# Moving eight weight-sum steps ahead of a bias load, and loading the bias in one transfer

## The chip, the cores and the metric

The kernel runs on one core of a Trainium2 chip. The metric is the device time of one execution in microseconds (us). Three timed runs of the kernel before the change stand beside one execution that was profiled; the times in the trace are counted from the start of its span.

## The reference

One layer of a transformer trunk on 512 tokens of width 2048, in float32: a norm, sliding-window attention with a learned bias by distance, an output projection, and a gated embedding. Cut to what matters here:

```python
hn = rmsnorm(x, norm_g)
q, k, v, gate = split(hn @ w_in)             # 32 query heads, 4 key heads, head width 64
bias = rel_bias[bucket(query - key)]         # 32 buckets x 32 heads
scores = q @ k.T * 64 ** -0.5 + bias         # a query sees 128 keys
probs = softmax over the seen keys and one sink per head
x = x + ((probs @ v) * silu(gate)) @ w_out
x = x + (p @ ple_proj) * sigmoid(rmsnorm(x) @ ple_gate)
return rmsnorm(x, final_g)
```

## The kernel before

Every float32 product is made from three matmuls on halves that TensorE takes at full rate: the high part of a weight times both parts of the activation, and the low part of the weight times the high part (`mm3`, L112, issued at L124 to L126). One step of such a product over 128 input channels is called a k-step here: three matmuls of 128x512.

The program has these stages. First the norm and the first columns of the input projection, one input block of 128 channels after the other (L177 to L246, tiles `xr`, `w0`, `w0s`, results `qps`, `ktps`, `vps`). Then the rest of the input projection, 30 column blocks of 16 k-steps each, run by a generator `proj`: the first 32 k-steps in a loop of four times eight, the others spread between the steps of the attention (L942 to L1008). Then the output projection, the gate and the last norm.

The weights of the generator come in pieces of 128x1024 (512 KB). `Weights.load` (L98) issues the read of a piece `wraw` on the queue of SP (the sync engine). ACT (ScalarE) rounds it to the high part `whi` (L107) and DVE (VectorE) subtracts to get `wlo` (L113). There are three buffers of each. A piece feeds eight k-steps, so 24 matmuls. Pieces are counted from 0 here; pieces 0 to 2 are read at the end of the first stage, and piece 3 is the first one behind the bias load on SP's queue.

The bias of the attention is a table by distance. POOL (GpSimd) reads `rel_bias` into the tile `misc` (L320), lays its columns out by distance with 17 copies (L324, L329), and writes the result to the DRAM tile `tdram` (L331). `load_bias(kv)` (L373) then reads the rows of one group of eight heads back, shifted per query, into the tile `bias`; `load_bias(0)` (L927) stands ahead of the first loop and waits for `tdram`, the others are issued inside the attention. The first use of the bias is `biased(0)` on DVE (L439).

The later projections use a scheme with fewer products that needs sums of weight blocks. They are made in DRAM during the attention by `sum_weights(i)` (L648): an even `i` issues a copy of a 512 KB block from DRAM to DRAM on SP's queue (L652), an odd `i` issues the accumulating transfer that adds a second block onto an earlier copy, on POOL's queue (L654), three copies behind. So of the steps 0 to 7, four issue copies (steps 0, 2, 4, 6) and one issues an accumulation (step 7). Below, C0, C1 ... are the copies and A0, A1 ... the accumulations, in their order; A0 waits until C0 has landed. Steps 0 to 7 stand in the first loop, two after every eight k-steps; the rest is spread over the attention.

The instruction order on TensorE and SP is that of the program text throughout. From the line ahead of `load_bias(0)` on, the order of POOL, DVE and ACT is the program's too; in the text ahead of it, which holds the building of the bias table, a scheduler orders those three by when it takes an instruction to be ready, and it may set instructions of the later text in front of earlier ones.

Of the kernel before, what the change touches and what calls it, by code (L numbers as in the profile page):

```python
# [20 lines left out]
P = 128  # L21
# [7 lines left out]
GROUP = HEADS // KVH  # L29
HB = P // 2  # L30
QB = P // GROUP
# [8 lines left out]
TOEP = 384  # L40
# [15 lines left out]
def trunk_kernel(ctx: ExitStack, tc: tile.TileContext, a: dict):  # L56
    nc = tc.nc
# [128 lines left out]
    for k in range(KC):  # L186
# [10 lines left out]
        h = room.tile([P, S], F32R, tag="ah", name=f"xh{k}")  # L197
# [127 lines left out]
    for b in range(exact, BUCKETS):  # L325
        d = np.nonzero(bk == b)[0]
        if len(d):
            lo, n = P - 1 + int(d.min()), len(d)
            nc.gpsimd.tensor_copy(tvec[:, lo : lo + n], relb[:, b : b + 1].to_broadcast([HEADS, n]))  # L329
    tdram = tc.dram_tile([HEADS, TOEP], F32, name="tdram")  # L330
# [12 lines left out]
    U, T, PT, O, gates, biases = {}, {}, {}, {}, {}, {}  # L343
# [28 lines left out]

    def load_bias(kv):  # L373
        biases[kv] = apool.tile([P, P + HB], F32, tag="bias", name=f"bias{kv}", bufs=2)
        for h in range(GROUP):
            src = bass.AP(
                tensor=tdram.tensor, offset=tdram.offset + (GROUP * kv + h) * TOEP + HB, ap=[[1, QB], [1, P + HB]]
            )
            nc.sync.dma_start(biases[kv][QB * h : QB * h + QB], src)

    def where(i):

# [4 lines left out]
    def scores(i):  # L387

        kv, j, g, s = where(i)
        if j == 8 and kv + 1 < KVH:
            load_bias(kv + 1)
        key = K[kv]
        q = Q[i // 4]
        s_ps = SP[i] = spsum.tile([P, 2, S], F32, tag="w", name=f"s{i}")
        n = (HB, P)[g] if g < 2 else P + QB
        for u in range(2):
            st = q[:, (2 * i + u) % (P // QB)].rearrange("p h q -> p (h q)")
            first = 0 if g < 2 else (g - 2) * HB + (s + u) * QB  # L400
            nc.tensor.matmul(s_ps[:, u, : 2 * n], st, key[:, :, first : first + n], start=True, stop=True)  # L401
# [214 lines left out]
    def large_sum(nm, p, only=range(2)):  # L616
        for jj in only:
            for m in range(4):
                first = {7: (1, 2), 5: (1, 1)}.get(p)
                summed[nm, p, jj, m] = sum_of(  # L620
                    block(nm, *first, jj, m) if first else summed[nm, 7 if p == 6 else 6, jj, m],
                    block(nm, *{7: (2, 2), 5: (1, 2), 6: (1, 1), 4: (2, 1)}[p], jj, m),
                    f"{nm}_{p}_{jj}_{m}",
                )
# [17 lines left out]
    large_sum("ple_gate", 5, (0,))  # L642
    small_sum(4, 4, lambda i: small[4, 6, i], lambda i: large_piece(1, 0, i))
    large_sum("ple_gate", 5, (1,))
    SUM_START = 8
    SUM_REST = 2 * len(copies) + 6 - SUM_START

    def sum_weights(i):  # L648

        if i % 2 == 0 and i // 2 < len(copies):  # L650
            if copies[i // 2]:
                nc.sync.dma_start(*copies[i // 2])  # L652
        elif i % 2 == 1 and 0 <= i // 2 - 3 < len(adds):
            nc.gpsimd.dma_start(*adds[i // 2 - 3], accum_op=ALU.add, max_dma_last_dim=8192)  # L654
# [247 lines left out]
    def projections():  # L902
# [21 lines left out]
            engines={getattr(mybir.EngineType, v) for v in ("PE", "SP", "Pool", "DVE", "Activation")}  # L924
        )
    )
    load_bias(0)  # L927
    blocks = KVH * STEPS
    at = 0

    def ksteps(n):
        nonlocal at
        for _ in range(n):
            while len(W.made) <= min(at // 8, len(W.srcs) - 1):
                W.split()
            at += 1
            next(proj)

    def splits(ahead):
        return len(W.made) <= min(at // 8 + ahead, len(W.srcs) - 1)  # L940

    for n in range(2 * 2):  # L942
        while splits(2):
            W.split()
        ksteps(8)
        for v in range(SUM_START // 4):
            sum_weights(n * (SUM_START // 4) + v)
    for e in range(2):
        for lo in (False, True):
            make_q(0, e, lo)  # L950
# [8 lines left out]
    for i in range(blocks + 3):  # L959
# [46 lines left out]
        if i < blocks:  # L1006
            for n in range(i * SUM_REST // blocks, (i + 1) * SUM_REST // blocks):
                sum_weights(SUM_START + n)  # L1008
    while W.open:
# [453 lines left out]
    n = done[3]  # L1463
# [87 lines left out]
```

## Time and profile before

| what | value |
|---|---|
| median of three timed runs | 791.01 us (790.99 to 791.08) |
| the profiled execution | 791.13 us |
| its span, first to last instruction | 789.4 us |
| mean granted TensorE clock | 0.998 |
| TensorE busy in the span | 779.7 us (99%) |
| VectorE, ScalarE, GpSimd busy | 613.5, 499.4, 174.4 us |
| HBM traffic over the span | 327 GB/s |

The profiled execution is 1.73 us longer than its span. Times in the trace are starts; "SPq" and "POOLq" are the queues from which an engine issues transfers. A transfer's time to landing runs from its issue to the moment the waiting engine may go on. Matmuls overlap: each has a duration of about 0.39 us in the trace while the next one starts 0.23 us after it, so starts are what counts.

### The profile page before, as it was taken

To read this page: it belongs to the slowest core of one execution; us is meant where nothing else is said; L and a number is where in the kernel's file an instruction comes from. 1 tells how busy PE (TensorE), PEld (TensorE's weight loads), DVE (VectorE), ACT (ScalarE), POOL (GpSimd) and SP (SyncE) were. 2 spreads that over 40 slices of the span, in tenths; PEclk is the share of its full clock that TensorE was granted. 3 is DMA by queue.
4 is the path that set the end of the run, shared out by engine and by line. 5 is a ranking of instruction groups with operands and counts; after the bars stand their busy time and mean duration, and the time that the engine had idled before them with its cause. 6 is when DMAs were issued, how large, how long until landed. Compare 5 with 4: busy or idle time off the path is not lost.

```text
span 789.4 us, 11241 instructions
## 1 busy us (share of the span) xinstructions
PE 779.7 (99%) x3738; PEld 651.6 (83%) x3738; DVE 613.5 (78%) x1043; ACT 499.4 (63%) x1015; POOL 174.4 (22%) x382
## 2 busy tenths in 40 slices
PE   9999999999999999999999999999999999999995
PEld 7888888888888888888888888888888888888885
DVE  4436478888877788687887798999788757899886
ACT  5632377667566666565666656767679756666755
POOL 0012413554244414542243200100000120200000
PEclk9999999999999999999999999999999999999999
DMA  8791999999999998999999597997783996885533
GB/s 336 276 225 41 315 279 289 253 300 282 327 277 268 255 276 242 240 256 278 281 282 220 154 321 252 269 380 265 239 298 101 358 225 227 163 215 192 178 107 107
DMA packets 48778, 194.41 MB, mean 246 GB/s; under 512 B 7328, under 2 KB 8480, under 8 KB 42992
## 3 DMA queue, kind: packets, MB, share of 16 engines
q1 hardware_dynamic: 39600, 148.81, 53.3%
q0 software_dynamic: 8688, 44.36, 29.7%
q8 instruction: 29, 0.48, 0.3%
q10 hardware_dynamic: 432, 0.52, 0.2%
q14 instruction: 29, 0.24, 0.1%
HBM read 187.85 MB, written 70.31 MB: 327 GB/s over the span
## 4 chain that ended last, share of the span: by engine, by line
PE 98%; DMA 1%; ACT 0%; DVE 0%; SPq 0%; issue 0%; ACTq 0%; DVEq 0%
PE gps L124 7%; PE gps L125 7%; PE gps L126 7%; PE qps L126 7%; PE qps L124 7%; PE qps L125 7%; PE o L125 6%; PE o L126 6%; PE o L124 6%; PE g L124 6%; PE g L125 6%; PE g L126 6%; PE s L401 2%; PE o L523 2%; PE vps L228 2%; PE pt L479 2%
## 5 line engine op out<-in xcount | busy, mean ns | idle before, releaser
L124 PE MATMUL gps<-xh,whi 128*128 128x512 f32 x256 | 100.4, 392 | 0.0
L125 PE MATMUL gps<-xl,whi 128*128 128x512 f32 x256 | 100.0, 391 | 0.0
L126 PE MATMUL gps<-xh,wlo 128*128 128x512 f32 x256 | 99.8, 390 | 0.0
L503 POOL TENSOR_SCALAR_AFFINE_SELECT own<-r 64x256 fp32r<-64x256 f32 x96 | 60.9, 634 | 165.1 <-ACT r L484 82.7
L113 DVE TENSOR_TENSOR wlo<-wraw,whi 128x1024 fp32r<-128x1024 f32 x60 | 74.0, 1235 | 24.0 <-ACT whi L107 22.5
L124 PE MATMUL qps<-xh,whi 128*128 128x512 f32 x224 | 87.5, 391 | 0.0
L125 PE MATMUL qps<-xl,whi 128*128 128x512 f32 x224 | 87.5, 390 | 0.0
L126 PE MATMUL qps<-xh,wlo 128*128 128x512 f32 x224 | 87.3, 390 | 0.0
L461 ACT ACTIVATE t<-t,sm 128x129 f32<-128x129 f32 x128 | 50.7, 397 | 49.6 <-DVE sm L452 46.8
L124 PE MATMUL g<-bhi,fhg 128*128 128x512 f32 x192 | 75.2, 391 | 0.0
L125 PE MATMUL g<-blo,fhg 128*128 128x512 f32 x192 | 74.7, 389 | 0.0
L126 PE MATMUL g<-bhi,flg 128*128 128x512 f32 x192 | 74.7, 389 | 0.0
L107 ACT CAST whi<-wraw 128x1024 fp32r<-128x1024 f32 x60 | 62.2, 1038 | 15.0 <-DMA wraw<-in_w_q 8.8
L689 ACT CAST bhi<-braw 128x1024 fp32r<-128x1024 f32 x44 | 46.3, 1054 | 36.0 <-PE g L126 19.4
L690 DVE TENSOR_TENSOR blo<-braw,bhi 128x1024 fp32r<-128x1024 f32 x44 | 54.0, 1228 | 18.6 <-ACT bhi L689 18.5
L690 DVE TENSOR_TENSOR blo<-ring,bhi 128x1024 fp32r<-128x1024 f32 x48 | 58.3, 1221 | 6.5 <-ACT bhi L689 6.1
L689 ACT CAST bhi<-ring 128x1024 fp32r<-128x1024 f32 x48 | 50.3, 1051 | 20.4 <-PE o L126 16.6
L484 ACT CAST r<-pt 128x256 fp32r<-128x256 f32 x64 | 23.8, 372 | 54.8 <-PE pt L479 54.4
L126 PEld LDWEIGHTS gps<-xh,wlo 128*128 128x128 f32 x256 | 48.1, 188 | 10.5
L124 PEld LDWEIGHTS gps<-xh,whi 128*128 128x128 f32 x256 | 48.1, 188 | 9.1
L125 PEld LDWEIGHTS gps<-xl,whi 128*128 128x128 f32 x256 | 48.1, 188 | 8.7
L671 POOL DMA_DIRECT2D grown<-in_ple_gate x16 | 13.7, 854 | 176.3 <-DMA grown<-ple_gate 119.7
(263 smaller groups left out, 1985.3 us busy)
## 6 DMA issues: line engine op xcount, KB each, us to landing
w_out<-in_w_out POOLq DMA_DIRECT2D x32, 512.0 KB, 8.6
wraw<-in_w_gate_in SPq DMA_DIRECT2D x32, 512.0 KB, 6.9
ring<-w_out SPq DMA_DIRECT2D x32, 512.0 KB, 5.5
wraw<-in_w_q SPq DMA_DIRECT2D x28, 512.0 KB, 8.3
braw<-in_ple_gate SPq DMA_DIRECT2D x24, 512.0 KB, 4.4
ring<-in_w_out SPq DMA_DIRECT2D x18, 512.0 KB, 4.5
w_out<-in_w_out SPq DMA_DIRECT2D x16, 512.0 KB, 9.1
w_out<-w_out SPq DMA_DIRECT2D x16, 512.0 KB, 13.5
```

The lines of the kernel that those rows point to most:

```text
L107: nc.scalar.copy(hi, self.raw[i])
L113: nc.vector.tensor_sub(lo, raw, hi.bitcast(F32))
L124: nc.tensor.matmul(ps, sh, mh, start=first, stop=False, skip_group_check=more)
L125: nc.tensor.matmul(ps, sh, ml, start=False, stop=False, skip_group_check=more)
L126: nc.tensor.matmul(ps, sl, mh, start=False, stop=last, skip_group_check=more)
L228: nc.tensor.matmul(v_ps[t], h[:, c], both[:, :, 256:512], start=f, stop=e, skip_group_check=True)
L401: nc.tensor.matmul(s_ps[:, u, : 2 * n], st, key[:, :, first : first + n], start=True, stop=True)
L461: nc.scalar.activation(su, su, AF.Exp, bias=sm[:, u : u + 1], accum_out=sm[:, 2 + u : 3 + u])
L484: nc.scalar.copy(r[:, 0], PT[i])
L503: nc.gpsimd.affine_select(out=cols(own[places[g % 2 ^ low]]), in_=cols(r[here, low].bitcast(F32)), pattern=[[sign * QB, 2], [0, GROUP], [s ...
L689: nc.scalar.copy(hi, raw)
L690: nc.vector.tensor_sub(lo, raw, hi.bitcast(F32))
```

## The change

`load_bias` issues one transfer for the 128 rows of a group where it issued eight of 16 rows each. Steps 0 to 7 of `sum_weights` go in front of `load_bias(0)`; the first loop issues steps 8 to 15 where it issued steps 0 to 7, and the part spread over the attention is shorter by eight steps.

```diff
     def load_bias(kv):
         biases[kv] = apool.tile([P, P + HB], F32, tag="bias", name=f"bias{kv}", bufs=2)
-        for h in range(GROUP):
-            src = bass.AP(
-                tensor=tdram.tensor, offset=tdram.offset + (GROUP * kv + h) * TOEP + HB, ap=[[1, QB], [1, P + HB]]
-            )
-            nc.sync.dma_start(biases[kv][QB * h : QB * h + QB], src)
+        src = bass.AP(
+            tensor=tdram.tensor, offset=tdram.offset + GROUP * kv * TOEP + HB, ap=[[TOEP, GROUP], [1, QB], [1, P + HB]]
+        )
+        nc.sync.dma_start(biases[kv], src)
...
-    SUM_START = 8
+    SUM_FIRST, SUM_START = 8, 16
     SUM_REST = 2 * len(copies) + 6 - SUM_START
...
+    for n in range(SUM_FIRST):
+        sum_weights(n)
     load_bias(0)
...
         ksteps(8)
-        for v in range(SUM_START // 4):
-            sum_weights(n * (SUM_START // 4) + v)
+        for v in range((SUM_START - SUM_FIRST) // 4):
+            sum_weights(SUM_FIRST + n * ((SUM_START - SUM_FIRST) // 4) + v)
```

The order of the instructions on TensorE, DVE and ACT is the same in both kernels. It differs on SP and on POOL.

SP's queue at the end of the first stage, before: three pieces of weights are read, then the bias, then pieces 3 and 4, and the copies of the weight sums (`small`) come after those.

```order
L101 DMA wraw_683<-in_w_q 128x1024
L379 DMA bias_810<-tdram 16x192 x8
L101 DMA wraw_823<-in_w_q 128x1024
L101 DMA wraw_829<-in_w_q 128x1024
L652 DMA small_7_0_746<-in_w_out 16x8192
L101 DMA wraw_861<-in_w_q 128x1024
L652 DMA small_7_1_747<-in_w_out 16x8192
```

The same place after (lines of the changed text are one or two lower):

```order
L101 DMA wraw_683<-in_w_q 128x1024
L651 DMA small_7_0_746<-in_w_out 16x8192
L651 DMA small_7_1_747<-in_w_out 16x8192
L651 DMA small_5_0_748<-in_w_out 16x8192
L651 DMA small_5_1_749<-in_w_out 16x8192
L378 DMA bias_815<-tdram 128x1x192
L101 DMA wraw_821<-in_w_q 128x1024
L101 DMA wraw_827<-in_w_q 128x1024
L651 DMA w_out_0_0_750<-in_w_out 16x8192
```

C0 to C3 stand ahead of the bias now, and the bias is one row instead of eight.

POOL at the same time, before: the spread of the norm's factors (`rb`), then the table in `misc`. Its write to `tdram` follows 13 rows further down, and A0 right behind that.

```order
L242 DMA rb<-rdram 128x512
L320 DMA misc<-in_rel 32x32
L321 MEMSET misc 32x384
L324 COPY misc<-misc 32x16
L329 COPY misc<-misc 32x3
L329 COPY misc<-misc 32x2
```

And after:

```order
L242 DMA rb<-rdram 128x512
L653 DMA small_7_0_746<-in_w_out 64x2048
L653 DMA small_7_1_747<-in_w_out 64x2048
L653 DMA small_5_0_748<-in_w_out 64x2048
L653 DMA small_5_1_749<-in_w_out 64x2048
L320 DMA misc<-in_rel 32x32
L321 MEMSET misc 32x384
L324 COPY misc<-misc 32x16
```

Four accumulations, A0 to A3, stand ahead of the building of the table. Only A0 belongs to the steps that the text puts in front of `load_bias(0)`; A1 to A3 come from the first loop, and the scheduler has set all four ahead of the read of `rel_bias`. The rest of the table is as before, and A4 follows the write to `tdram` where A0 followed it.

## The prediction

> **What bounds the kernel now.** I read the page's busy shares and chain first, then the windows around the changed place, then SP's waits and the timelines of SP, POOL, ACT, DVE and PE between 49 and 105 us.
>
> ```profile
> PE 779.7 (99%) x3738; PEld 651.6 (83%) x3738; DVE 613.5 (78%) x1043; ACT 499.4 (63%) x1015; POOL 174.4 (22%) x382
> PE 98%; DMA 1%; ACT 0%; DVE 0%; SPq 0%; issue 0%; ACTq 0%; DVEq 0%
> ```
>
> TensorE is busy for 779.7 of 789.4 us and carries 98% of the chain. No transfer and no other engine holds it up anywhere between the first load and the tail. So nothing that only shortens work on SP, POOL or the DMA engines can shorten the run; a step that makes TensorE wait lengthens it by that wait.
>
> The windows (columns PE, PEld, DVE, ACT, POOL busy, granted clock, DMA share, GB/s) show what lies fallow at the changed place:
>
> ```profile
> 59.00:60.00 1.00, 1.00 (x6) 0.78 (x6) 1.00 (x2) 1.00 (x2) 1.00 (x1) 1.00 0.25 102
> 60.00:65.00 5.00, 5.00 (x25) 4.21 (x24) 4.08 (x5) 2.19 (x3) 4.64 (x6) 1.00 0.00 2
> 65.00:70.00 5.00, 5.00 (x25) 4.17 (x24) 1.76 (x5) 0.00 (x0) 0.00 (x0) 1.00 0.06 13
> 70.00:75.00 5.00, 5.00 (x26) 4.17 (x25) 4.95 (x11) 1.65 (x3) 0.00 (x0) 1.00 0.06 14
> ```
>
> The DMA engines run dry at about 59.25 (a quarter of that us) and stand still to 75 while TensorE goes on at full clock. SP's waits and its queue say why:
>
> ```profile
> SPq L379 <- DMA tdram<-misc: 14.8, 1, 14.8
> SPq L379 <- PE vps L228: 5.3, 1, 5.3
> 49.58 1.81 SPq L101 DMA_DIRECT2D wraw<-in_w_q  x3
> 71.69 3.88 SPq L379 DMA_DIRECT2D bias<-tdram  x8
> 75.60 0.90 SPq L101 DMA_DIRECT2D wraw<-in_w_q  x2
> 76.55 0.60 SPq L652 DMA_DIRECT2D small<-in_w_out  x1
> ```
>
> SP is free at 51.39, waits 14.8 us for the table (to 66.2), then 5.3 us for the last `vps` matmul, whose weights lie where the bias goes. Piece 3 of the weights is queued behind that bias.
>
> **The slack of piece 3.** PE's first matmul on piece 0, its first on piece 3, and the split of piece 3:
>
> ```profile
> 71.49 0.40 PE L124 MATMUL qps<-xh,whi 128*128 128x512 f32 x1
> 87.83 0.39 PE L124 MATMUL qps<-xh,whi 128*128 128x512 f32 x1
> 79.59 1.05 ACT L107 CAST whi<-wraw 128x1024 fp32r<-128x1024 f32 x1 [5.98 <-DMA wraw<-in_w_q]
> 80.67 1.23 DVE L113 TENSOR_TENSOR wlo<-wraw,whi 128x1024 fp32r<-128x1024 f32 x1 [4.82 <-ACT whi L107]
> ```
>
> 72 matmuls take 16.34 us, 0.227 each. Piece 3 is issued at 75.60, lands at 79.5 (3.9 later), `wlo` is done at 81.9 (2.4 later). PE wants `wlo` with its third matmul, 0.45 after the first, so piece 3 is ready for a start at 81.45 and is wanted at 87.83: 6.4 us of slack.
>
> **The change part by part.** The bias in one transfer:
>
> ```profile
> L379 SPq DMA_DIRECT2D bias<-tdram x32: 302/418/676, 71.7 to 308.5; - x32
> ```
>
> Eight issues took 3.88 us; for one I take the median of 0.42 (least 0.30, most 0.68). It gives piece 3 some 3.4 us. The later three bias loads save issue time on SP too, and since PE waits for nothing there, that is worth nothing. Steps 8 to 15 in place of 0 to 7 and the shorter rest: the same instructions earlier, on queues PE does not wait for; nothing.
>
> The copies in front: C0 to C3 go out from 51.39 on, while SP would only wait, so their issue costs nothing. What they cost lies on POOL. A0 to A3 stand ahead of the table there, each waits for its copy, and behind them wait the table, `tdram`, the bias on SP and piece 3. POOL before:
>
> ```profile
> 49.71 0.53 POOL L320 DMA_DIRECT2D misc<-in_rel  x1
> 57.40 0.19 POOL L324 COPY misc<-misc 32x16 f32<-32x16 f32 x1 [6.73 <-DMA misc<-in_rel]
> 64.42 0.51 POOL L331 DMA_DIRECT2D tdram<-misc  x1 [0.29 <-POOL misc L329]
> 83.67 0.86 POOL L654 DMA_DIRECT2D small<-in_w_out  x1 [18.74 <-DMA wraw<-in_w_q]
> ```
>
> Step one, the copies. Three transfers in a row (C0, piece 5, C1, issued at 76.55, 77.19, 77.81) landed after
>
> ```profile
> DMA to landing us min/median/max: 6.8/6.8/6.8
> DMA to landing us min/median/max: 7.6/7.6/7.6
> DMA to landing us min/median/max: 8.0/8.0/8.0
> ```
>
> that is at 83.35, 84.79 and 85.81: one per 1.23 us. Starting at 59.25 with about 1 us to land, C0 lands at 61.5, and alone C1 to C3 would at 62.7, 64.0, 65.2; their data are out at 64.2. POOL took A0 up 0.3 us after C0 landed (83.67). So A0 is issued at 61.8, and A3 at about 66.
>
> Step two, the accumulations. They come one after the other on POOL's transfer queue. The trace has a stretch where little else ran than such transfers (into SBUF, L671, window 630 to 650, columns packets, MB, share of 16 engines):
>
> ```profile
> q0 software_dynamic: 1077, 3.95, 99.6%
> q0 software_dynamic: 8688, 44.36, 29.7%
> ```
>
> 19.9 us for 3.95 MB is 2.64 us per block of 0.524 MB; over the whole run (second row) it is 2.77. I take 2.7, nearest to both. With 0.86 us of issue and some 0.8 to the first byte (an estimate: the 5.1 us that the quickest of the L671 transfers needs, less 0.86, 2.64 and 0.8 to land), A0 moves from 63.4. Then 0.85 us of copies and 4 x 2.7 us of accumulations are left for the same DMA engines: done at 75.05, landed at 75.95.
>
> ```profile
> DMA to landing us min/median/max: 5.1/5.3/5.4
> rb<-rdram POOLq DMA_DIRECT2D x1, 256.0 KB, 7.6
> misc<-in_rel POOLq DMA_DIRECT2D x1, 4.0 KB, 7.6
> ```
>
> Step three, the table. `misc` is 4 KB, and still needed 7.6 us behind the 256 KB `rb` issued 0.57 us before it: it landed 0.57 after `rb`. I read that as a queue that goes in order. So `misc` lands at 76.5, not 57.4. From there to `tdram` landing took 8.8 us (57.4 to 66.2): 85.3. The bias adds 0.42; piece 3 is issued at 85.75, lands at 89.65, and is ready for a start at 91.6. PE wants it at 87.83: it waits 3.8 us.
>
> **Sum.** In short, wait = landing of `misc` - 72.75, and nothing below 72.75. 789.4 + 3.8 = 793.2 of span, with 1.73 around it 794.9 for the profiled execution; from the median of 791.01, 0.12 lower, 794.8.
>
> What is late next: A4 stands behind `tdram` on POOL and waits for C4, now behind pieces 3 and 4 on SP. C0 was issued 0.95 after piece 3 and landed 6.8 later; so C4 lands at 93.5.
>
> ```profile
> 88.88 0.74 POOL L355 TENSOR_TENSOR values<-values 64x256 f32<-64x256 f32 x1
> 100.18 0.76 DVE L302 TENSOR_TENSOR diffs<-diffs 128x256 fp32r<-128x256 f32 x2 [0.53 <-ACT diffs L301]
> ```
>
> From A0's start to the end of the key differences POOL took 5.95 us (83.67 to 89.62), so they are done at 99.5; DVE wants them at 100.18 + 3.8 = 104. That cover of 4.5 us holds. Piece 4 lands some 1.5 us behind piece 3 and is wanted 5.4 behind it. No second wait.
>
> **A page against a row.** The Trainium skill (DMA: Bandwidth & Descriptors, "Anatomy of one DMA — SWDGE (gpsimd) path") prices a POOL transfer at 2.0 us plus its bytes at 436 GB/s. By that a block moves in 1.2 us once the first is under way (an estimate from that page), the sum would be no wait and 791.0, and the change would be free. The row of 2.64 us is what this kernel measured for accumulating transfers, and I go by it.
>
> **The rivals.** *B, no wait.* The accumulations run at the pace of plain transfers, 1.23 us, or `misc` isn't held by them. Then A3, issued at 65.5, moves at 67.2 and is landed at 69.2; `misc` lands at 69.8, 3 us inside the point of 72.75. Everything stays hidden: 791.0. It decides where one accumulation costs under some 1.8 us. For it speaks that the queues are empty between 60 and 75, against it the 2.64. The page's rule above would make this the outcome. Chance 0.15.
>
> *C, a long wait and the clock.* Copies and accumulations disturb each other: were the copies to need 2.64 each as well, work would end at 59.25 + 8 x 2.64 = 80.4, `misc` land at 81.9 and PE wait 9.1 us. The clock then matters. After the last matmul, at 780.5, the windows have
>
> ```profile
> 784.00:785.00 1.00, 0.00 (x0) 0.00 (x0) 0.86 (x3) 0.59 (x1) 0.00 (x0) 1.00 0.54 176
> 785.00:786.00 1.00, 0.00 (x0) 0.00 (x0) 0.00 (x0) 0.13 (x1) 0.00 (x0) 0.94 1.03 345
> 786.00:787.00 1.00, 0.00 (x0) 0.00 (x0) 0.00 (x0) 0.00 (x0) 0.00 (x0) 0.50 1.05 357
> 780.54 0.28 PE L126 MATMUL e<-bhi,pTl 128*128 128x256 f32 x1
> 0.85 3.66 PE L145 MATMUL warm_ps<-const-bfloat16-1.0 128*128 128x128 bf16 x34 [0.85 <-PEq L1541]
> ```
>
> a full clock for 5.1 us and half of it from 785.9 on. How long it stays at half, no row shows; the warm-up of 3.66 us at the start is the nearest, and half a clock for that long loses 1.8. In the forecast PE stands idle for 2.7 us, then 0.8 for `wlo`, and the clock holds. With `misc` at 79.3 the wait is 6.5 and the clock goes: 791.0 + 6.5 + 1.8 = 799.3. At 9.1 it would be 801.9. Chance 0.10. The Trainium skill (TensorE: Matmul & The Clock Gate, "What's actually happening") puts the fall after one idle window of about 3.4 us, earlier than the 5.1 seen here; by it a wait only little above my forecast would already pay.
>
> *D, faster.* Merged bias issues and earlier sums would have to free time on PE. There is none to free in the rows. Chance 0.03, for something not in the profile.
>
> **How the numbers follow.** The forecast (wait of 1.6 to 6) has 0.72 and gives 794.8. About 0.2%, 1.6 us, is what a measurement of this kernel tells from no change; B lies within it, D below, the forecast and C above: faster 0.03, same 0.15, slower 0.82. Low is 790.9, since B is cheap to reach and the accumulations' price, 1.23 to 2.77, spans 791 to 795.1; high is 800.0, C at its likelier place.
>
> **What would show it.** Right: POOL's first L324 copy near 76.5, `bias` issued on SP near 85.3, a gap of 3 to 4 us in PE's row near 88, with the releaser `whi` or `wlo`, and all PE starts behind it late by that much, the DMA share near 1 from 60 to 75. Wrong: L324 before 72.7 (B), a PEclk below 1 near 90 (C), a first L324 as early as 57, or a second PE gap between 95 and 115 (POOL's key differences).

## The result and the profile after

The changed kernel takes 793.73 us (median of 7 runs, 792.72 to 793.87) beside 791.09 for the kernel before on the same chip (7 runs, 790.99 to 791.74): 1.0027 of its time, interval 1.0017 to 1.0037, so 2.6 us slower. The profiled execution took 793.84 us with a span of 792.1, 2.7 more than before. Its busy times and its chain:

```profile
PE 781.3 (99%) x3738; PEld 652.4 (82%) x3738; DVE 614.4 (78%) x1043; ACT 499.2 (63%) x1015; POOL 168.5 (21%) x382
PE 87%; DMA 7%; DVE 2%; ACT 1%; SPq 1%; issue 1%; POOL 0%; ACTq 0%; DVEq 0%; POOLq 0%
```

TensorE is as full as before, but the chain runs through DMA and DVE for 9%. Followed through the changed place, it goes by C3, the read of `misc` (10.2 us), `tdram`, the bias, piece 5 (8.5 us) and piece 9 (12.0 us) to a matmul at 132.60. The windows at the changed place (PE, PEld, DVE, ACT, POOL busy, granted clock, DMA share, GB/s):

```profile
60.00:65.00 5.00, 5.00 (x25) 4.17 (x24) 3.63 (x4) 1.94 (x3) 2.19 (x3) 1.00 0.86 272
65.00:70.00 5.00, 5.00 (x26) 4.17 (x25) 1.47 (x5) 0.00 (x0) 1.96 (x4) 1.00 0.92 172
70.00:75.00 5.00, 5.00 (x26) 4.18 (x25) 4.95 (x11) 1.65 (x3) 0.00 (x0) 1.00 0.96 197
75.00:80.00 5.00, 5.00 (x24) 4.14 (x23) 1.15 (x4) 0.00 (x0) 2.75 (x18) 1.00 0.04 7
```

The DMA engines, empty there before, work on the sums until 75. POOL's timeline (start, duration, engine, line, operation, and in brackets the idle time before it with its releaser):

```profile
61.89 0.85 POOL L653 DMA_DIRECT2D small<-in_w_out  x1 [11.44 <-DMA small<-in_w_out]
65.70 0.77 POOL L653 DMA_DIRECT2D small<-in_w_out  x1 [0.49 <-DMA small<-in_w_out]
66.21 0.80 POOL L320 DMA_DIRECT2D misc<-in_rel  x1
76.54 0.19 POOL L324 COPY misc<-misc 32x16 f32<-32x16 f32 x1 [9.10 <-DMA misc<-in_rel]
76.67 2.08 POOL L329 COPY misc<-misc 32x3 f32<-32x3 f32 x16
79.05 0.54 POOL L331 DMA_DIRECT2D tdram<-misc  x1 [0.30 <-POOL misc L329]
```

A0 and A3 stand at 61.89 and 65.70, and the 4 KB of `misc` land at 76.54, behind all four accumulations. SP's queue and the two steps of piece 3 behind it:

```profile
81.02 0.72 SPq L378 DMA_DIRECT2D bias<-tdram  x1
81.80 0.87 SPq L101 DMA_DIRECT2D wraw<-in_w_q  x2
82.72 0.55 SPq L651 DMA_DIRECT2D w_out<-in_w_out  x1
86.13 1.05 ACT L107 CAST whi<-wraw 128x1024 fp32r<-128x1024 f32 x1 [12.23 <-DMA wraw<-in_w_q]
87.22 1.23 DVE L113 TENSOR_TENSOR wlo<-wraw,whi 128x1024 fp32r<-128x1024 f32 x1 [11.07 <-ACT whi L107]
```

Piece 3 goes out at 81.80, 6.2 us later than before, against a slack of 6.4; `wlo` is done at 88.45 and PE takes it at about 88.5. Here it comes just in time. TensorE's waits between 80 and 140 us lie elsewhere:

```profile
PE o L522 <- DVE r L491: 0.6, 1, 0.6
PE o L524 <- POOL own L502: 0.3, 1, 0.3
121.91 0.39 PE L522 MATMUL o<-r,V 128*128 128x256 f32 x1 [0.58 <-DVE r L491]
132.60 0.39 PE L524 MATMUL o<-own,DV 128*128 128x256 f32 x1 [0.26 <-POOL own L502]
```

Matmul by matmul, starts after less starts before, PE is 0.3 late from the first loads on, loses 0.3 at 97.5, 0.9 at 120.65 and 0.9 at 130.3 (times of before), and no more than 0.1 up to its last matmul; the rest of the 2.7 comes in the tail. The two steps of 0.9 are larger than the waits in the rows, since weight loads wait there as well. They lie in the attention, 30 us and more behind the place where the wait was expected.

### The profile page after: what moved, and what is told of

Same layout as the page of the kernel before. It is cut to its first block, busy times and chain, and to the rows that moved or that the text cites. A ratio compares the mean times of both kernels' runs of the same rounds, so it can differ in the third digit from the quotient of the medians.

```text
span 792.1 us, 11202 instructions
## 1 busy us (share of the span) xinstructions
PE 781.3 (99%) x3738; PEld 652.4 (82%) x3738; DVE 614.4 (78%) x1043; ACT 499.2 (63%) x1015; POOL 168.5 (21%) x382
## 4 chain that ended last, share of the span: by engine, by line
PE 87%; DMA 7%; DVE 2%; ACT 1%; SPq 1%; issue 1%; POOL 0%; ACTq 0%; DVEq 0%; POOLq 0%
PE gps L124 7%; PE gps L125 7%; PE gps L126 7%; PE o L125 6%; PE o L126 6%; PE o L124 6%; PE g L124 6%; PE g L125 6%; PE g L126 5%; PE qps L124 5%; PE qps L125 5%; PE qps L126 5%; DMA wraw<-in_w_q 3%; PE s L400 2%; PE o L522 2%; PE pt L478 2%
```

## The experiments

Times are medians beside runs of the kernel before on the same chip (791.43 of 24 runs for the first four, 791.47 of 29 for the others), with the interval of the ratio.

**The bias in one transfer alone.** The kernel before with the new `load_bias`, and the sums where they were.

```diff
-        for h in range(GROUP):
-            ...
-            nc.sync.dma_start(biases[kv][QB * h : QB * h + QB], src)
+        src = bass.AP(
+            tensor=tdram.tensor, offset=tdram.offset + GROUP * kv * TOEP + HB, ap=[[TOEP, GROUP], [1, QB], [1, P + HB]]
+        )
+        nc.sync.dma_start(biases[kv], src)
```

> Only the first half of the change: the bias read in one transfer, the sums where they were. Theory Q (the queue behind the table: the time goes where POOL builds the table late and SP, held by it, issues weights and copies late): 791.1 as before, at most 0.3 away, since PE waits for nothing there; piece 3 is issued near 72.4 instead of 75.6. Rival M (the merged transfer itself is the slower one): 792.5 or more, with a piece of weights landing late behind it.

Measured 791.44, ratio 1.0 (0.9991 to 1.0009). Piece 3 goes out earlier (72.75 for 75.60), and by itself that is worth nothing: PE did not wait for it.

**The sums in front, the bias still in eight.** The changed kernel with the old loop in `load_bias`, the reverse of the diff above.

> Only the other half: the sums in front, the bias still in eight transfers. Theory Q: the table lands as in the changed kernel (tdram near 81.0), eight issues take about 3.9 where one took 0.7, so piece 3 comes 3.2 later than in the changed kernel, where it was just in time: PE waits about 3 us near 88, and the rest of the chain shifts too, 795.5 to 797. Rival D (the earlier copies and accumulations crowd the transfers, whatever waits for whom): 793.7 as the changed kernel, since the same bytes move. Rival M: 791.1.

Measured 797.43 (5 runs, 796.64 to 799.96), ratio 1.0078 (1.0062 to 1.0094). SP's queue, PE, and two windows:

```profile
82.46 3.57 SPq L379 DMA_DIRECT2D bias<-tdram  x8
91.49 0.72 PE L124 MATMUL qps<-xh,whi 128*128 128x512 f32 x1 [2.98 <-ACT whi L107]
91.00:92.00 1.00, 0.51 (x1) 0.43 (x2) 0.53 (x1) 0.44 (x1) 0.00 (x0) 0.80 1.55 512
93.00:94.00 1.00, 1.00 (x3) 0.81 (x4) 0.87 (x3) 0.46 (x1) 0.00 (x0) 0.50 1.27 528
```

The wait of the forecast is here, 2.98 us for `whi` of piece 3, and behind it the granted clock is 0.50: matmuls start 0.43 apart until 95.04, and PE, 3.7 us late at the first of them, is 5.6 late at the last. The time is 0.4 above the range given, which had no fall of the clock in it. The second place costs 0.45 us more, at 136.4. So the merged bias, worth nothing alone, saves the changed kernel some 3.7 us (797.43 less 793.7): it is only worth something where the sums have used up the slack.

**The table first.** The changed kernel, with POOL held to the order of the text from the table on, so that the table stands ahead of A0 to A3 again. Copies and accumulations are as early as the text puts them.

```diff
     misc = quarter("misc")
     ...
+    during = ExitStack()
+    during.enter_context(tc.manual_schedule(engines={mybir.EngineType.PE, mybir.EngineType.SP, mybir.EngineType.Pool}))
     nc.gpsimd.dma_start(relb, a["rel"])
```

> The changed kernel with POOL kept in program order from the table on: the table is built and written first, and A0 to A3 follow it; PE, DVE, ACT and SP keep the changed kernel's order. Theory Q: misc lands near 57, SP issues the bias near 71.5, PE has no wait at 97, 121 and 132, and the time is 791.1 (790.8 to 791.5). Rival D: copies and accumulations move as early or earlier, so 793 to 794 stays. Rival M: 793 to 794 stays too.

Measured 791.55, ratio 1.0 (0.9991 to 1.0009). POOL:

```profile
57.41 0.19 POOL L326 COPY misc<-misc 32x16 f32<-32x16 f32 x1 [5.94 <-DMA misc<-in_rel]
57.54 6.60 POOL L331 COPY misc<-misc 32x3 f32<-32x3 f32 x16
64.94 3.32 POOL L655 DMA_DIRECT2D small<-in_w_out  x4
```

The lines are two higher here. `misc` lands at 57.41 as before, A0 to A3 go out behind the table, PE has no new wait and the loss is gone. Four copies, four early accumulations and one bias transfer cost nothing; the order on POOL costs all of it.

**A4 later.** Step 15, which issues A4, leaves the first loop for the attention. POOL then goes from the table straight to the key differences, with no wait for C4 between. The steps behind it move with it: C8 goes out behind the first spreads of the differences (106.14; 95.12 in the changed kernel), and A7 at 106.12 (101.32).

```diff
-    SUM_FIRST, SUM_START = 8, 16
+    SUM_FIRST, SUM_START = 8, 15
...
-        for v in range((SUM_START - SUM_FIRST) // 4):
-            sum_weights(SUM_FIRST + n * ((SUM_START - SUM_FIRST) // 4) + v)
+        for v in range(2):
+            if SUM_FIRST + 2 * n + v < SUM_START:
+                sum_weights(SUM_FIRST + 2 * n + v)
```

> The changed kernel without the last step of the first loop (A4), which moves with the steps behind it into the attention, behind the key differences on POOL. The table is as late as in the changed kernel. If the late table costs by POOL's second wait (A4 waits for a copy queued behind the bias, and holds the differences, the first tiles and A5 to A7, which then collide with the spread of the differences and a weight piece): differences done near 88, A4 to A6 near 91 to 94, no waits of PE at 121 and 132, 791.1 to 791.9. If SP's own lateness suffices (pieces and copies behind the late bias): 793 to 794 as the changed kernel.

Measured 793.70 (8 runs, 791.65 to 796.02), ratio 1.0026 (1.0011 to 1.0041). The key differences start at 81.45 and the waits at 121 and 132 are gone, but in this execution `misc` landed at 78.40, 1.9 later than in the other, and PE shows

```profile
89.01 0.50 PE L124 MATMUL qps<-xh,whi 128*128 128x512 f32 x1 [0.77 <-ACT whi L107]
90.27 0.50 PE L126 MATMUL qps<-xh,wlo 128*128 128x512 f32 x1 [0.53 <-DVE wlo L113]
```

at full clock, 1.9 us in all. The second place is cured and the first one pays, so the 791.1 to 791.9 that were expected for a cure are missed. The cure is less certain here than it looks: a PE that is 2 us late would also hide part of a wait at 121 and 132.

**The bias behind pieces 3 and 4.** `load_bias(0)` moves into the first loop, behind its first reads of weights, so that a late table can't hold piece 3.

```diff
-    load_bias(0)
...
             W.split()
+        if n == 0:
+            load_bias(0)
         ksteps(8)
```

> The changed kernel with the first bias load moved behind pieces 3 and 4 on SP's queue; POOL, PE, DVE and ACT keep the changed kernel's order, so the table is as late (misc near 77 to 79) and A4 still stands ahead of the key differences. If the loss has two places, piece 3 behind the bias (0 to 2 us, from run to run) and POOL's wait for C4 (about 2 us at 121 and 132): pieces 3 and 4 land before 70, no PE wait near 88 in any run, the second place stays, 793 to 794.5. If piece 3 alone carried it: 791.4.

Measured 794.38 (12 runs, 793.09 to 799.11), ratio 1.0034 (1.002 to 1.0047). Pieces 3 and 4 go out at 59.61 and 61.61 (piece 4 lands at 75.1, later than expected) and nothing waits at 88; the two waits in the attention are there:

```profile
121.76 0.39 PE L522 MATMUL o<-r,V 128*128 128x256 f32 x1 [0.26 <-DVE r L491]
132.45 0.39 PE L524 MATMUL o<-own,DV 128*128 128x256 f32 x1 [0.26 <-POOL own L502]
```

The first place is cured and the second one pays.

**Both.** The two edits together.

> Both cures at once: the first bias load behind pieces 3 and 4, and A4 behind the key differences. Table and A0 to A3 as in the changed kernel. If those two places are the whole of it: no PE wait at 88, 121 or 132, 791.4 (791.0 to 792.0), the time of before. If the earlier transfers cost in another way: 792.5 or more.

Measured 792.08 (12 runs, 791.20 to 797.71), ratio 1.0016 (1.0001 to 1.0031). In the profiled execution, with a span of 790.4, PE waits at none of the three places, and its end is 0.7 late, all of it from the first 13 us. `misc` lands at 81.41 there, 4.9 us later than in the changed kernel, so a late table alone does not make PE wait. What the median keeps, 0.6 us (0.1 more than the range given), and two runs of 795.82 and 797.71 have no trace and stay open.

**The changed kernel again.**

> The changed kernel once more, beside the others on their chip: 793.7 (792.7 to 794.5). With the table near 76.5 piece 3 is ready within 0.3 us of the moment that PE wants it, so its wait should differ from execution to execution; the waits at 121 and 132 should be there again.

Measured 793.82 (12 runs, 792.61 to 796.25), ratio 1.0027 (1.0017 to 1.0037). The profiled execution is the slowest of them, 796.25, and pays at the other place. POOL, PE and windows:

```profile
79.66 0.19 POOL L324 COPY misc<-misc 32x16 f32<-32x16 f32 x1 [10.61 <-DMA misc<-in_rel]
90.22 0.50 PE L124 MATMUL qps<-xh,whi 128*128 128x512 f32 x1 [1.77 <-ACT whi L107]
91.48 0.79 PE L126 MATMUL qps<-xh,wlo 128*128 128x512 f32 x1 [0.53 <-DVE wlo L113]
88.00:89.00 1.00, 0.45 (x2) 0.02 (x1) 0.00 (x0) 0.00 (x0) 0.00 (x0) 1.00 0.98 164
90.00:91.00 1.00, 0.73 (x2) 0.30 (x2) 0.80 (x1) 0.17 (x1) 0.00 (x0) 1.00 1.14 352
91.00:92.00 1.00, 0.52 (x1) 0.50 (x2) 1.00 (x3) 0.00 (x0) 0.00 (x0) 0.66 1.04 430
94.00:95.00 1.00, 1.00 (x4) 0.76 (x4) 0.41 (x1) 0.22 (x1) 1.00 (x4) 0.64 0.42 172
```

`misc` lands 3.1 us later than in the first execution, PE waits 1.8 and 0.5 us for piece 3, and the clock halves besides: 4.4 us lost at this place, and no wait at 121 and 132, as it seems because a PE that is 4.4 us late there comes after what it waited for. In these two executions one kernel pays at one place or the other; `misc`, which landed at 76.54 in one and 79.66 in the other, decides whether it pays at the first.

**Twice as many in front.** 16 steps ahead of `load_bias(0)`, so that eight accumulations stand ahead of the table.

```diff
-    SUM_FIRST, SUM_START = 8, 16
+    SUM_FIRST, SUM_START = 16, 24
```

> Sixteen steps in front of the bias load instead of eight: eight copies on SP, and A0 to A7 on POOL ahead of the table. With 2.7 us for an accumulation and 1.23 for a copy, misc lands at 63.4 + 5.7 + 8 x 2.7 and 1.5 to land, near 92; with the 4.5 us that the table takes when DVE is idle, piece 3 comes 15 to 16 us too late; the clock goes to half for about 3.4 us (1.7 more): 791.4 + 16 + 1.7 = 809 (806 to 812). If the accumulations were not in each other's way (rival: misc is held by the copies' landing, not by the queue), misc would land near 80 and the time be 797 to 799.

Measured 810.74 (4 runs, 810.10 to 811.97), ratio 1.0242 (1.0226 to 1.0257).

```profile
93.49 0.19 POOL L324 COPY misc<-misc 32x16 f32<-32x16 f32 x1 [15.02 <-DMA misc<-in_rel]
103.84 0.79 PE L124 MATMUL qps<-xh,whi 128*128 128x512 f32 x1 [15.96 <-ACT whi L107]
92.00:93.00 1.00, 0.00 (x0) 0.00 (x0) 0.00 (x0) 0.00 (x0) 0.00 (x0) 0.62 0.10 18
109.00:110.00 1.00, 1.00 (x5) 0.79 (x5) 1.00 (x1) 0.00 (x0) 0.93 (x2) 0.85 1.28 520
```

`misc` lands 17.0 us later than in the first execution of the changed kernel, and 13.8 us later than in the second (79.66), for four more copies and four more accumulations; the prediction's prices, 4 x (1.23 + 2.7), give 15.7, which lies between. The rival, `misc` near 80 by the copies' landing alone, falls. The clock costs more than the 1.7 us expected: by the last two rows it is at half from 92.24 to 109.30, so that PE works at half clock for 5.5 us and loses 2.9 beside the wait.

## Why the prediction was right, and where not

**The direction and the first links of the chain: right.** The table first takes all of the loss away, twice the sums multiply it. Of the signs that the prediction gave, `misc` near 76.5 and DMA engines at work up to 75 came. The bias near 85.3 (it went out at 81.02) and the gap of 3 to 4 us near 88 did not come in the profiled execution, where the loss lies at a place that the prediction had cleared. Rival B (no wait, the queue at the pace of plain transfers) falls with `misc` at 76.5, not 69.8, and with it, for accumulating transfers, the rule of the Trainium skill (DMA: Bandwidth & Descriptors, "Anatomy of one DMA — SWDGE (gpsimd) path") that stood beside it. D (faster) falls with a merged bias that is worth nothing alone.

**The landing of `misc`: right to 0.1 us in this execution**, 76.5 for 76.54. Other executions of kernels with the same sums in front had 77.98, 78.40 and 79.66 (80.60 and 81.41 where pieces 3 and 4 went ahead as well), so the hit is partly luck. The 1 us that the sum gave a copy to land had no row behind it; A0, issued at 61.89 for 61.8, bears out the sum up to there. Whether the order of POOL's queue holds `misc` back, as the prediction read it, or the load of the DMA engines (0.92 and 0.96 in the windows from 65 to 75), no run separates: a read of `rel_bias` on another queue was not tried.

**From `misc` to `tdram`: the term that was mis-sized.** 8.8 us were taken over from before; it took 4.5 (76.54 to 81.02). The 16 copies took 2.08 us instead of the 6.61 that they took before. Rows of before show why; first DVE, then POOL's copies one by one:

```profile
58.85 1.23 DVE L113 TENSOR_TENSOR wlo<-wraw,whi 128x1024 fp32r<-128x1024 f32 x1 [2.94 <-ACT whi L107]
59.99 0.95 DVE L208 TENSOR_TENSOR w0s<-w,w0s 128x768 fp32r<-128x768 f32 x1
57.53 6.61 POOL L329 COPY misc<-misc 32x3 f32<-32x3 f32 x16
58.89 1.23 POOL L329 COPY misc<-misc 32x10 f32<-32x10 f32 x1
60.07 0.92 POOL L329 COPY misc<-misc 32x10 f32<-32x10 f32 x1
```

A copy of 32x10 that begins beside a DVE subtraction ends with it, after 0.92 or 1.23 us; with DVE idle, 16 of them take 2.08, 0.13 each. At 76.7 DVE had nothing to do (its last operation began at 75.67). The same copies took 6.60 us in the kernel with the table first, at the same place as before, and 2.07 in the one with sixteen steps in front. The Trainium skill (SBUF — State Buffer, "Who interferes with whom") says that a DVE instruction with two SBUF inputs contends with a GpSimd instruction that reads SBUF, and calls the contention an exclusive lock; these rows agree. The bias's issue was a term the other way, 0.72 us for 0.42, and the landing of piece 3 took 4.3 for 3.9. Together piece 3 is ready at 88.0 instead of 91.6, on the edge: a wait of 0 in one execution, of 2.3 and a halved clock in another.

**"No second wait": wrong.** The cover of 4.5 us rested on PE being 3.8 late, and it priced the key differences but not what stands behind them on POOL. What happened, POOL after:

```profile
90.97 0.83 POOL L653 DMA_DIRECT2D w_out<-in_w_out  x1 [11.39 <-DMA w_out<-in_w_out]
97.33 1.07 POOL L355 TENSOR_TENSOR values<-values 64x256 f32<-64x256 f32 x1
99.62 0.79 POOL L653 DMA_DIRECT2D w_out<-in_w_out  x1
101.32 0.93 POOL L653 DMA_DIRECT2D w_out<-in_w_out  x1
```

A4 waits for C4, which SP issued at 82.72 behind the late bias, until 90.97. The key differences end at 98.40, and A5 to A7 follow in a lump from 99.62 to 101.32. Before, the next three accumulations stood at

```profile
90.83 0.79 POOL L654 DMA_DIRECT2D small<-in_w_out  x1
93.86 0.77 POOL L654 DMA_DIRECT2D small<-in_w_out  x1 [1.13 <-DMA small<-in_w_out]
```

and the last of them landed at 105.7, 2.3 us after SP had sent piece 9 behind the spreads of the differences (`DV`). In the changed kernel the spreads, piece 9 and C9 meet the lump: A7 lands at 113.1, 7.5 us after piece 9 is sent. The rows are SP's read of piece 9, ACT's rounding of it, and the time to landing of C9, issued at 106.37:

```profile
105.61 0.71 SPq L101 DMA_DIRECT2D wraw<-in_w_q  x1
117.64 1.05 ACT L107 CAST whi<-wraw 128x1024 fp32r<-128x1024 f32 x1 [2.23 <-DMA wraw<-in_w_q]
DMA to landing us min/median/max: 12.3/12.3/12.3
```

Piece 9 is taken 12.0 us after its issue. Before, ACT had not waited for it at all. ACT, DVE behind it (`r`) and POOL (`own`) become late, and those are the two waits of PE. The prediction had named a second gap between 95 and 115 as a sign against it; apart from the 0.3 us at 97.5 it came at 121 and 132.

That the place of the sums behind the late table causes them is shown by "both" beside "the bias behind": the waits go when A4 is moved. But C8 and A7 move with A4 there, so it is not shown that A4's place alone does it. That the lump is what slows piece 9 is read from the order of events and was not tried by itself. A rival would be that piece 9 is only sent late (2.2 us later than before), since the chain reaches it through piece 5, which is late behind the bias. The rows speak against it; piece 9 at ACT in "the bias behind", where it was sent at 104.56, and in "both", where it was sent later, at 105.03:

```profile
117.48 1.05 ACT L107 CAST whi<-wraw 128x1024 fp32r<-128x1024 f32 x1 [2.49 <-DMA wraw<-in_w_q]
115.09 1.05 ACT L107 CAST whi<-wraw 128x1024 fp32r<-128x1024 f32 x1
```

In the five traces where ACT waits for piece 9 (both executions of the changed kernel, the bias in eight, the bias behind, sixteen in front), the last accumulation ahead of it lands 6.4 to 8.6 us after piece 9 is sent; in the five where ACT does not wait (before, the bias in one transfer, the table first, A4 later, "both"), 1.7 to 3.6 us after.

**"The clock holds" below a wait of some 5 us: wrong.** The prediction read a fall 5.1 us after the last matmul as the limit. It fell after a gap of 3 us (bias in eight), and after gaps of 1.8 and 0.5 with two matmuls between them (the changed kernel again), not after 0.8 and 0.5 (A4 later). So C's mechanism works at waits that C thought safe. The size of half-clock time, guessed from the warm-up's 3.66 us, was near in the changed kernel: from the windows, with clocks of 0.66 and 0.64 in the first and the last, 91.3 to 94.7, 3.4 us; with the bias in eight it was 3.4 us too (91.6 to 95.0). With sixteen steps in front it was 17.06 us. The Trainium skill (TensorE: Matmul & The Clock Gate, "What's actually happening") gives a window of 3413 ns that runs on freely, and a fall after one idle window. The 3.4 us are one such window and the 17.06 five. By an estimate from that page a fall lies between one and two windows, 3.4 to 6.8 us, after the last matmul, and the 5.1 of the end lies there. Here the measurement differs, and decides: with the bias in eight the clock fell at 91.6, 3.1 us after the last matmul's end (88.12 and 0.39). The window before a fall need not be idle: in the changed kernel the 3.4 us up to 91.3 held some 1.3 us of matmul work (0.1 ahead of 88, 0.45 from 88 to 89, 0.73 from 90 to 91).

So 794.8 came out near 793.7 by two errors that largely cancel: the table 4.3 us cheaper than thought, and a second place and the clock that were thought free. The number is in part luck.

## What to carry to other kernels

Before work is put in front of a late step, list everything that the same queue holds behind it: here a 4 KB read took its turn behind four accumulating transfers, and through it a table, a bias and a weight piece. A duration taken over from the trace of before holds only if its neighbours move with it; look at what the other engines did in that stretch. Where slack has just been used up, the same program may pay at different places from run to run, and curing one of them may bring nothing until the next is cured too.

## What was not expected of the hardware

- 16 small POOL copies took 6.61 us beside DVE subtractions and 2.08 alone.
- The clock halved for 3.4 us after a stretch in which TensorE stood for 1.8 and 0.5 us, and cost about 2 us on top of the wait there and with the bias in eight, 2.9 with sixteen steps in front, where it was at half for five times as long.
- One transfer for 128 rows of bias took 0.72 us to issue, where one for 16 rows had a median of 0.42: 0.72 against 3.57 to 3.88 for eight.
- Four copies and four accumulations issued some 20 us earlier (A0 at 64.94 for 83.67 with the table first) cost TensorE nothing, as long as nothing that it waits for stood behind them.
